# Sample tile in pairs and quads of 128-column chunks per PSUM bank, and one PSUM bank held back instead of two, in a four-layer hybrid decoder step

## The chip, the cores and the metric

The kernel runs on all 8 cores of one Trainium2 chip. Each core holds one prompt of 2048 positions and one tile of 128 sample positions (16 sequences of 8). The cores do not talk to each other. The time of a run is the device time of its slowest core, in microseconds (us).

A run has a state. In the fast state all cores have about the same granted TensorE clock (in nearly all of them 0.985 to 0.994 of full speed). In the slow state the cores of one die, sometimes of both, have a lower one, here down to 0.81, and the run is some per cent longer. I use a second figure, called the **die median** below: of every run, take each die (cores 0 to 3, 4 to 7) whose four cores all had a granted clock above 0.985, take the median span of its four cores, and then the median over all such dies. An undisturbed die in a slow run is as good as one in a fast run: of the kernel before, 28 dies of fast runs have a median of 6847.9 us, and 15 undisturbed dies of slow runs one of 6847.5. For the kernel before, this figure came out as 6847.1, 6847.7, 6847.0 and 6850.8 us (8 to 12 dies each, three chips), so it repeats within 4 us, 0.06%.

## The reference

Each of 4 layers does this, for the prompt and for the sample alike:

```python
h = rmsnorm(x, n1) * (1 + sc1) + sh1
x = x + 0.5 * gt1 * swiglu(h, f1g, f1u, f1d)            # "FFN1", width 2816
h = rmsnorm(x, nm) * (1 + sc2) + sh2
xp, xl, gl, u, v, gates = split(h @ w_in)
y_pool = pool_mixer(xp)                                  # windows 2, 4, 8, 16
y_lru  = rg_lru(causal_conv(xl)) * gelu(gl)              # conv of width 4, gates, a recurrence
y_gm   = chunk_gmlp(u, v)                                # positions mixed in chunks of 128
g = sigmoid(gates)
x = x + gt2 * ((g0*(y_pool@wbo_pool) + g1*(y_lru@wbo_lru) + g2*(y_gm@wbo_gmlp)) @ w_out)
h = rmsnorm(x, n2) * (1 + sc3) + sh3
x = x + 0.5 * gt3 * swiglu(h, f2g, f2u, f2d)            # "FFN2"
```

A last RMSNorm follows. The model width is 1024, which the kernel holds as 8 chunks of 128 channels on the partitions, with the positions along the free axis. The new states of pooling, conv, RG-LRU and gMLP are outputs too.

## The kernel before

The work comes in two passes. The first takes half of the prompt, the second takes the other half with the sample tile riding along:

```python
GROUPS = [
    [TT_("p", 0, 512, 0), TT_("p", 512, 512, 512)],
    [TT_("p", 0, 512, 1024), TT_("p", 512, 512, 1536), TT_("s", 1024, 128, 0)],
]
```

The kernel declares its PSUM buffer as `[P, 8, 512]` in fp32, and its planner hands it out as 8 banks of 512 values. A prompt tile has 512 columns and fills one bank. A sample tile has 128 columns and leaves three quarters of its bank empty. This is what the FFN does for each of 22 hidden chunks and for every tile, the sample included:

```python
def unit(wb, jb, ji, t):
    ...
    pg, pu = PV(), PV()                       # two banks
    acc(pg.c(n), [(g[:, k, ji * P:(ji + 1) * P], hT[:, k, t.cols]) for k in range(KC)], n)
    acc(pu.c(n), [(u[:, k, ji * P:(ji + 1) * P], hT[:, k, t.cols]) for k in range(KC)], n)
    sg = SB()
    act(sg.f(n), pg.c(n), AF.Silu)
    tt(hid(jb * 2 + ji)[:, t.cols], sg.f(n), pu.c(n), ALU.mult)
```

The branch gates, the pooling input, the down and output projections with their residual, and the RMSNorm sums follow the same pattern: one chunk, one bank, one ACT and one DVE instruction. The two gates of an RG-LRU chunk take a bank each:

```python
for t in grp:                                  # in Lru.gates
    pr, pi = PV(), PV()
    acc(pr.c(n), [(wr_, hb.b(n, t.col))], n)
    acc(pi.c(n), [(wi_, hb.b(n, t.col))], n)
    act(self.ab.f(n, t.col), pr.c(n), AF.Tanh, bias=lruc[:, l, 2, ch:ch + 1], scale=0.5)
    act(self.ib.f(n, t.col), pi.c(n), AF.Tanh, bias=lruc[:, l, 3, ch:ch + 1], scale=0.5)
```

No engine's order is written by hand. When the program is built, a planner plays the whole program through with cost figures of its own, and each time an engine is free it takes the first instruction, in program order, that is ready *and fits*. `fits` decides on PSUM banks and on pages of a scratch area in SBUF. The order on each engine, the banks and the pages are then fixed for good. These are the parts that the argument touches:

```python
SEM_LAT = 70.0                                 # planner: end of an instruction to its dependant, ns

def place(vb):                                 # a run of free scratch pages of 64 floats
    ...
    down = not w and vb.nu <= 9                # small buffers from the top, larger ones from below
    ...

def fits(o):
    ...
    if need and len(banks) < need + (0 if first else 2):
        return False                           # an instruction out of turn must leave 2 banks free
    ...
```

`first` is true where the instruction's bank is the next in program order. An instruction that is not the next one may only take a bank if two more stay free. In the trace every TensorE instruction (PE) has the one source line of the helper that recorded it, L623, or L624 after the change; DVE and ACT lines are those of helpers likewise. Groups are therefore told apart by their operands: `R` are the large activations (FFN hidden, pooled and gated branches), `mem` is scratch or weights, `onesb` is the ones matrix of the norm sums.

Of the kernel before, what the change touches and what calls it, by code (L numbers as in the profile page):

```python
# [13 lines left out]
ALU = mybir.AluOpType  # L14
# [19 lines left out]
LRU_LEAD = 1.3  # L34

# [92 lines left out]
class Sched:  # L128
# [103 lines left out]
    def schedule(self):  # L232
# [60 lines left out]
        def fits(o):  # L293
# [9 lines left out]
            if need and len(banks) < need + (0 if first else 2):  # L303
                return False
# [206 lines left out]
def build_nc():  # L511
# [306 lines left out]
    class Norm:  # L818
# [8 lines left out]
        def chunk(self, m):  # L827
            t, n = self.t, self.t.n
            x = self.x(m)
            if m == 0:  # L830
                self.sum = SB(n)
                act(self.sum.f(n), x, AF.Square)
            else:
                sq = SB(n)
                act(sq.f(n), x, AF.Square)
                if m < KC - 1:
                    tt(self.sum.f(n), self.sum.f(n), sq.f(n), ALU.add)
                else:
                    tot = SB(n // 2)
                    tt(tot.b(n), self.sum.f(n), sq.f(n), ALU.add)  # L840
                    mm([(self.pv.c(n), onesb[:], tot.b(n), True, True)], n)
            self.k += 1
# [28 lines left out]
    def final_norm(nm):  # L871
        t, n = nm.t, nm.t.n
        r = nm.rstd()
        for k in range(KC):
            y = SB()
            stt(y.f(n), xT[:, k, t.cols], vecT[:, V_NF + k:V_NF + k + 1], r.f(n), ALU.mult, ALU.mult)
            if t.kind == "p":
                dma(y_p[:, k, t.pos0:t.pos0 + n], y.f(n))
            else:
                dma(y_s[:, k, :], y.f(n))  # L880

    def resid(l, wh, m, t, pv):
        n = t.n
        xs_ = xT[:, m, t.cols]
        if t.kind == "p":
            stt(xs_, pv.c(n), modp(l, wh, m), xs_, ALU.mult, ALU.add)
        else:
            tmp = SB()
            g3 = modT[:, l % 2, wh * 8 + m, 1:17].unsqueeze(2).to_broadcast([P, NSEQ, TSAMP])
            tt(tmp.f(n).rearrange("p (s t) -> p s t", t=TSAMP),  # L890
               pv(lambda b: b[:, 0:n].rearrange("p (s t) -> p s t", t=TSAMP)), g3, ALU.mult, n=n)
            tt(xs_, xs_, tmp.f(n), ALU.add)
# [5 lines left out]
    def ffn(l, which, grp, after, between=None, begin=None):  # L898
# [4 lines left out]
        def unit(wb, jb, ji, t):  # L903
            n = t.n
            g = w3(wb[:, 0:2048], KC)
            u = w3(wb[:, 2048:4096], KC)
            pg, pu = PV(), PV()
# [25 lines left out]
        def down(wb, m, t):  # L933
            n = t.n
            w = w3(wb, NJ)
            py = PV()
            acc(py.c(n), [(w[:, j, :], hid(j)[:, t.cols]) for j in range(NJ)], n)
            resid(l, wh, m, t, py)
            norms[id(t)].chunk(m)

        for m in range(4):
            v = wload(dn[l, m], NJ * P)
            for t in grp:
                down(v, m, t)
            hook()
# [3 lines left out]
        for t in grp:  # L949
            for m in range(4, KC):  # L950
                down(vs[m - 4], m, t)
            after(norms[id(t)])


    def gate_unit(l, br, wblk, nk, m, grp, src):
# [3 lines left out]
        tot = sum(t.n for t in grp)  # L959
        sg = SB(tot)  # L960
        for t in grp:
            n = t.n
            pp, pg = PV(), PV()
# [4 lines left out]
            if br == 0:  # L968
                stt(merged[:, m, t.cols], s_, 1.0, pp.c(n), ALU.add, ALU.mult)
            else:  # L970
                stt(s_, s_, 1.0, pp.c(n), ALU.add, ALU.mult)
        if br != 0:
            mg = merged[:, m, 0:tot]
            tt(mg, mg, sg.f(tot), ALU.add)

    def window(d, x, w, carry, smp=False):

        n = NSEQ * 23 if smp else NPR
        pick = (lambda a: a.rearrange("p (s x) -> p s x", s=NSEQ)[:, :, 15:23]) if smp else (lambda a: a)
        m = P if smp else NPR  # L980
# [16 lines left out]
    def pool_unit(l, g, grp, wblk, gi):  # L997
        wv = wblk
        w = 2 << g
        last = gi == len(GROUPS) - 1  # L1000
        wx = w3(wv[:, 0:2048], KC)
        for c in range(2):
# [7 lines left out]
            xs = None  # L1010
            for t in grp:
                n = t.n
                pb = PV()
                acc(pb.c(n), [(wx[:, k, c * P:(c + 1) * P], hT[:, k, t.cols]) for k in range(KC)], n)
                if t.kind == "p":
                    act(x[:, 16 + t.col:16 + t.col + n], pb.c(n), AF.Copy)
                else:
                    xs = SB(16 + NSEQ * 23)
                    x3 = xs.f(NSEQ * 23, 16)
                    memset(xs.f(16), 0.0)  # L1020
                    dma(x3, spool_d[l, ch])
                    act(x3.rearrange("p (s x) -> p s x", s=NSEQ)[:, :, 15:23],
                        pb(lambda b: b[:, 0:P].rearrange("p (s x) -> p s x", s=NSEQ)), AF.Copy, n=n)
                    dma(o_pool_s[l, ch], x3)
# [5 lines left out]
            if xs is not None:  # L1030
                window(ybr[:, ch, NPR:NPR + P].rearrange("p (s x) -> p s x", s=NSEQ), xs.f(16 + NSEQ * 23), w, False, True)
# [3 lines left out]
    class Lru:  # L1035
# [9 lines left out]
        def gates(self):  # L1045
# [37 lines left out]
            for t in grp:  # L1083
                n = t.n
                pr, pi = PV(), PV()
                acc(pr.c(n), [(wr_, hb.b(n, t.col))], n)
                acc(pi.c(n), [(wi_, hb.b(n, t.col))], n)
                act(self.ab.f(n, t.col), pr.c(n), AF.Tanh, bias=lruc[:, l, 2, ch:ch + 1], scale=0.5)
                act(self.ib.f(n, t.col), pi.c(n), AF.Tanh, bias=lruc[:, l, 3, ch:ch + 1], scale=0.5)
# [37 lines left out]
    def gm_v(l, t, sub, wblk):  # L1127
# [10 lines left out]
        act(vnb, pv.c(512), AF.Copy, scale=sm[:, 1:2])  # L1138
        if t.kind == "s":
# [3 lines left out]
            dma(o_v_s[l], vf.f(512))  # L1143

    def gm_u(l, t, g, wblk):
        n = t.n
        nsub = n // P
        wu3 = w3(wblk, KC)
        wm = wsp[:, g if t.kind == "p" else 4 + g, :]
        px = PV()  # L1150
        mm([(px(lambda b, s=s: b[:, s * P:(s + 1) * P]),
             vnT[:, (t.col + s * P) * 4 + g * P:(t.col + s * P) * 4 + (g + 1) * P], wm, True, True)
            for s in range(nsub)], P)
        sb_ = SB()
        b3 = bsb[:, 0 if t.kind == "p" else 1, g, :].unsqueeze(1).to_broadcast([P, nsub, P])
        stt(sb_.f(n).rearrange("p (s x) -> p s x", x=P), px(lambda b: b[:, 0:n].rearrange("p (s x) -> p s x", x=P)),
            vcol(l, "gn", g), b3, ALU.mult, ALU.add, n=n)
        pu = PV()
        acc(pu.c(n), [(wu3[:, k, g * P:(g + 1) * P], hT[:, k, t.cols]) for k in range(KC)], n)
        tt(ybr[:, g, t.cols], pu.c(n), sb_.f(n), ALU.mult)  # L1160

    def mixer(l, grp, gi, after):
# [66 lines left out]
        for g in range(4):  # L1229
            for t in grp:  # L1230
                fg.append((2.0 * t.n / 512, lambda t=t, g=g: u_f(t, g)))
# [22 lines left out]
        for t in grp:  # L1254
            nm = Norm(t)
            for m in range(KC):
                n = t.n
                py = PV()
                wo = w3(wos[m // 2], KC)
                acc(py.c(n), [(wo[:, k, (m % 2) * P:(m % 2 + 1) * P], merged[:, k, t.cols]) for k in range(KC)], n)  # L1260
                resid(l, 5, m, t, py)
# [28 lines left out]
    def first_norm(grp, x=None):  # L1290
        for t in grp:
            nm = Norm(t, x)
            for m in range(KC):
# [163 lines left out]
```

## Time and profile before

The kernel before took 6863.71 us (median of 3 runs, 6861.04 to 7466.54). Its profiled run fell in the slow state. These are lines of the profile's list of cores, before:

```profile
core 5: 6834.7 us, clock 0.989
die 0 (median of its cores): 7025.1 us, clock 0.958
die 1 (median of its cores): 6847.9 us, clock 0.988
```

Die 1 was undisturbed, so all that follows is read from core 5. This is its busy line from the profile page (busy time, share of the span, instructions), and the line of the page for the slowest core that says which engine the chain that ended last ran through:

```profile
PE 6608.6 (97%) x37553; PEld 3221.1 (47%) x37553; DVE 3000.5 (44%) x4419; ACT 2481.4 (36%) x3988; POOL 659.6 (10%) x1257
PE 88%; issue 4%; DVE 3%; ACT 2%; DMA 2%; POOL 1%; SPq 0%; DVEq 0%; ACTq 0%; POOLq 0%
```

TensorE bounds the kernel, and DVE and ACT are less than half busy on average. I therefore looked for a gain only where PE is idle. The next fence shows layer 2 of the second pass in three stretches of the windows view, core 5, before: the mixer with its output projection, FFN2, and FFN1 of the next layer. The cuts are at the norm-sum matmuls of those boundaries.

```profile
core 5: us, PE busy (x) PEld busy (x) DVE busy (x) ACT busy (x) POOL busy (x), PEclk, DMA share, GB/s
4403.60:4754.30 350.70, 327.18 (x1927) 164.57 (x1926) 223.60 (x301) 170.30 (x282) 59.91 (x102) 0.97 0.40 77
4754.30:5013.00 258.70, 255.70 (x1547) 130.88 (x1546) 83.31 (x158) 67.17 (x124) 9.51 (x18) 0.99 0.35 64
5013.00:5299.10 286.10, 286.10 (x1785) 148.49 (x1784) 96.47 (x177) 85.72 (x149) 14.87 (x32) 1.00 0.40 74
```

In FFN1 the PE is busy in 286.10 of 286.10 us. In FFN2 it loses 3.0 us, all at its start. The mixer loses 23.5 us, with DVE at 64% and ACT at 49%.

The ends of matmuls are modelled, which hides short gaps: a 128-column matmul is shown as 220 ns long, while the next one starts 56 ns after it. I therefore also sum, over the second pass, how much later each matmul starts after the one before it than at full rate. Full rate is what the trace shows within runs of matmuls: 216 ns between starts for 512 columns, 56 ns for 128 (the small 17-column ones, which occur in the first pass only, are counted at 30 ns, though most follow at 25). I call that sum the **excess**. Before, it was 172.8 us for the second pass on core 5.

These are the largest waits of the PE for ACT or DVE in the second pass, before (columns: engine, its line, what was waited for; us in total, times, longest):

```profile
PE psum L623 <- ACT mem L645: 59.2, 49, 4.7
PE psum L623 <- DVE R L653: 24.6, 12, 3.7
PE psum L623 <- DVE mem L653: 21.9, 7, 7.3
```

The longest wait of the first line, 4.7 us, is not in a mixer. It stands in the FFN1 at the start of the second pass (PE timeline, before, window 3262:3284):

```profile
3276.11 8.26 PE L623 MATMUL psum<-hT,mem 128*128 128x512 bf16 x36 [4.75 <-ACT mem L645]
```

There an ACT eviction of the sample tile had waited 10.5 us for a transfer of first-pass results (`y_p`), and for some 6 us after the wait the matmuls started 427 ns apart (mean granted clock 0.57 between 3276 and 3283 us). The excess of this place is 7.7 us, called the **stall at the start of the pass** below.

What one instruction of the sample tile costs is in the list of groups by shape, before (count | busy us, mean ns | idle before it). The first two lines are a sample chunk's eviction on ACT and a sample chunk's product on DVE, the third is the same product of a prompt tile, and the last counts the table loads of ACT:

```profile
L645 ACT ACTIVATE mem<-psum 128x128 f32<-128x128 f32 x381 | 107.0, 283 | 357.4 <-PE psum L623 323.2 <-DVE R L653 14.4 <-DMA y_p<-mem 10.5
L653 DVE TENSOR_TENSOR R<-mem,psum 128x128 bf16<-128x128 f32 x176 | 50.7, 288 | 56.2 <-PE psum L623 30.3 <-ACT mem L645 25.7
L653 DVE TENSOR_TENSOR R<-mem,psum 128x512 bf16<-128x512 f32 x704 | 483.2, 688 | 1857.7 <-PE psum L623 1754.1 <-ACT mem L645 103.3
L645 ACT ACT_TABLE_LOAD x257 | 329.7, 1283 | 206.9 <-PE psum L623 172.6 <-DVE small L653 9.0 <-DVE R L653 5.4
```

A product of 128 columns takes 288 ns and one of four times as many takes 688. If a straight line joins the two, some 155 ns of each are fixed: an estimate. The same estimate for ACT, from 283 ns for 128 columns and 598 for 512 (`ACTIVATE mem<-psum 128x512`, x1524), is some 178 ns. Two waits repeat in each of the four mixers. The first is the PE's timeline at the start of FFN2, before (start us, duration us, instruction, count, and in brackets the idle time before it with its releaser):

```profile
4754.49 13.65 PE L623 MATMUL psum<-R,mem 128*128 128x512 bf16 x104
4771.14 0.59 PE L623 MATMUL psum<-mem,onesb 128*128 128x512 bf16 x1 [3.00 <-DVE mem L653]
```

After the last output projection (104 matmuls), the PE waits 3.00 us until DVE has added up the squares for the norm. The second is the PE's timeline where the gMLP branch meets the RG-LRU gates, before:

```profile
4600.26 0.22 PE L623 MATMUL psum<-wsp,R 128*128 128x128 bf16 x1
4604.19 1.97 PE L623 MATMUL psum<-mem 128*128 128x512 bf16 x5 [3.70 <-DVE R L653]
```

A position-mixing matmul of the sample (`wsp`) is followed by 3.70 us of nothing before the matmuls of the RG-LRU gates.

### The profile page before, as it was taken

The numbers are of one execution on the slowest core, as the hardware profiler recorded it, in microseconds if no ns is written. First come the engines' busy times: TensorE is split into PE (matmuls) and PEld (weight loads), VectorE is DVE, ScalarE is ACT, GpSimd is POOL, SyncE is SP. The second block draws the span as 40 slices with busy tenths as digits, with TensorE's granted clock in tenths as the row PEclk, the third lists the DMA queues.
The fourth block names the chain that finished last, engine by engine and source line by source line (L and its number), as shares of the span: only waits on it lengthen the run. The fifth ranks groups of instructions, "written<-read, shape, count | busy, mean of one in ns | idle before, by whom it ended". The sixth has DMA issues, their size and how long they took to land.

```text
span 7032.5 us, 105309 instructions; the slowest of 8 cores (6834.7 to 7032.5 us)
## 1 busy us (share of the span) xinstructions
PE 6808.5 (97%) x37553; PEld 3267.9 (46%) x37553; DVE 3001.3 (43%) x4419; ACT 2478.3 (35%) x3988; POOL 654.7 (9%) x1257
## 2 busy tenths in 40 slices
PE   7999999999999999999999999999999999999999
PEld 3434444444444444444454455544455444554444
DVE  2254321653327422653427533275332754327543
ACT  3253221542226312543326332164321543215431
POOL 0011000110002000110002100011000110001100
PEclk8878888999999999999999999999999999999999
DMA  6566545665555556554634334343333333344333
GB/s 125 85 109 101 90 80 96 111 105 100 103 104 107 95 93 120 108 96 82 143 57 97 69 59 80 62 86 70 66 71 74 79 72 66 63 77 86 70 63 71
DMA packets 165357, 613.90 MB, mean 87 GB/s; under 512 B 22128, under 2 KB 58224, under 8 KB 125424
## 3 DMA queue, kind: packets, MB, share of 16 engines
q0 software_dynamic: 101376, 530.62, 43.4%
q1 hardware_dynamic: 63472, 76.55, 3.7%
q8 instruction: 312, 5.11, 0.3%
q14 instruction: 197, 1.61, 0.1%
HBM read 1103.15 MB, written 30.34 MB: 161 GB/s over the span
## 4 chain that ended last, share of the span: by engine, by line
PE 88%; issue 4%; DVE 3%; ACT 2%; DMA 2%; POOL 1%; SPq 0%; DVEq 0%; ACTq 0%; POOLq 0%
PE psum L623 88%; ACT mem L645 1%; DVE mem L690 1%; DMA mem<-ada_w 1%; DVE mem L668 1%; DMA mem<-ffn_gu 1%; ACT L645 1%; DMA mem<-w_v 0%; DVE mem L653 0%; POOL small L653 0%; DMA y_p<-mem 0%; DVE R L668 0%; DVE R L653 0%; ACT R L645 0%; POOL small L661 0%
## 5 line engine op out<-in xcount | busy, mean ns | idle before, releaser
L623 PE MATMUL psum<-hT,mem 128*128 128x512 bf16 (+1 forms) x22400 | 4398.5, 356 | 50.7 <-ACT mem L645 37.0
L623 PEld LDWEIGHTS psum<-hT,mem 128*128 128x128 bf16 x22400 | 2041.0, 100 | 2271.3 <-issue 535.2
L623 PE MATMUL psum<-R,mem 128*128 128x512 bf16 (+1 forms) x11520 | 2269.3, 354 | 41.9 <-ACT mem L645 17.7
L645 ACT ACTIVATE mem<-psum 128x512 f32<-128x512 f32 (+1 forms) x1969 | 1023.9, 536 | 2989.9 <-PE psum L623 2744.4
L623 PEld LDWEIGHTS psum<-R,mem 128*128 128x128 bf16 x11520 | 1049.1, 99 | 1177.9 <-issue 240.6
L653 DVE TENSOR_TENSOR R<-mem,psum 128x512 bf16<-128x512 f32 (+1 forms) x880 | 533.6, 607 | 2010.2 <-PE psum L623 1887.6
L645 ACT ACTIVATE mem<-xT 128x512 f32<-128x512 f32 (+1 forms) x504 | 279.2, 561 | 1121.8 <-DVE xT L668 1065.0
L668 DVE SCALAR_TENSOR_TENSOR xT<-psum,modT,xT 128x512 f32<-128x512 f32 x384 | 286.2, 750 | 728.5 <-PE psum L623 728.3
L645 ACT ACT_TABLE_LOAD x257 | 329.7, 1283 | 235.5 <-PE psum L623 181.1
L668 DVE SCALAR_TENSOR_TENSOR mem<-mem,psum 128x512 f32<-128x512 f32 x320 | 194.0, 607 | 457.2 <-PE psum L623 454.3
L653 DVE TENSOR_TENSOR mem<-mem 128x512 f32<-128x512 f32 (+3 forms) x471 | 284.7, 612 | 201.3 <-ACT mem L645 193.3
L698 POOL DMA_DIRECT2D mem<-ffn_gu x176 | 93.0, 529 | 2399.3 <-PE psum L623 2335.9
L645 ACT ACTIVATE hT<-mem,modT 128x512 bf16<-128x512 f32 x384 | 276.1, 801 | 52.1 <-DVE mem L653 33.1
L668 DVE SCALAR_TENSOR_TENSOR mem<-mem,vecT 128x1024 f32<-128x1024 f32 (+1 forms) x288 | 273.2, 974 | 8.0
L653 DVE TENSOR_TENSOR mem<-xT,mem 128x512 f32<-128x512 f32 x392 | 252.0, 688 | 52.1 <-ACT mem L645 42.6
L668 DVE SCALAR_TENSOR_TENSOR mem<-mem 128x1024 f32<-128x1024 f32 (+1 forms) x128 | 163.8, 1285 | 194.2 <-ACT mem L645 193.9
L645 ACT ACTIVATE mem<-mem 128x512 f32<-128x512 f32 (+3 forms) x209 | 187.5, 899 | 10.4 <-DVE R L653 4.2
L698 POOL DMA_DIRECT2D mem<-ffn_dn x128 | 67.6, 529 | 1279.8 <-PE psum L623 1261.7
L645 ACT ACTIVATE mem<-psum,lruc 128x128 f32<-128x128 f32 (+1 forms) x320 | 172.4, 631 | 39.3 <-DVE mem L690 15.7
L653 DVE TENSOR_TENSOR R<-R,mem 128x1024 bf16<-128x1024 bf16 (+1 forms) x128 | 165.3, 1291 | 13.6 <-DVE mem L668 0.9
L645 ACT ACTIVATE mem<-mem,lruc 128x1024 f32<-128x1024 f32 (+1 forms) x128 | 165.5, 1293 | 10.4 <-DVE mem L668 6.3
L690 DVE TENSOR_TENSOR_SCAN mem<-mem,lrust 128x1024 f32<-128x1024 f32 (+1 forms) x64 | 158.8, 2481 | 3.6 <-DVE mem L653 0.3
(77 smaller groups left out, 1959.4 us busy)
## 6 DMA issues: line engine op xcount, KB each, us to landing
mem<-ffn_gu POOLq DMA_DIRECT2D x176, 1024.0 KB, 9.5
mem<-ffn_dn POOLq DMA_DIRECT2D x128, 704.0 KB, 6.9
mem<-ada_w POOLq DMA_DIRECT2D x72, 1024.0 KB, 10.2
mem<-w_gate POOLq DMA_DIRECT2D x32, 1024.0 KB, 10.0
mem<-w_gate POOLq DMA_DIRECT2D x32, 768.0 KB, 8.3
mem<-w_lru POOLq DMA_DIRECT2D x64, 320.0 KB, 7.1
mem<-w_pool POOLq DMA_DIRECT2D x32, 512.0 KB, 9.4
mem<-w_lru POOLq DMA_DIRECT2D x64, 256.0 KB, 9.2
```

What stands on the lines that cost most here:

```text
L623: ins = e.matmul(res(o), lhsT=res(l), rhs=res(r), start=st, stop=sp)
L645: return S.add("act", lambda e: e.activation(out=res(out), in_=res(in_), func=func, **kw), reads=rd, writes=wr, cost=cost, tset=TSETS.get( ...
L653: return S.add(eng, lambda e: e.tensor_tensor(out=res(out), in0=res(in0), in1=res(in1), op=op), reads=[in0, in1], writes=[out], cost=dcost(n))
L668: return S.add(eng, lambda e: e.scalar_tensor_tensor(out=res(out), in0=res(in0), scalar=scalar, in1=res(in1), op0=op0, op1=op1), reads=rd, ...
L690: return S.add("dve", lambda e: e.tensor_tensor_scan(out=res(out), data0=res(d0), data1=res(d1), initial=init, op0=op0, op1=op1), reads=rd ...
L698: return S.add(q, lambda e: e.dma_start(out=res(out), in_=res(in_), **kw), reads=[in_] if reads is None else reads, writes=[out] if writes ...
```

## The change

The intent is twofold. First, the sample tile is worked on two chunks at a time (or two gates and two values, or all four gMLP groups), side by side in one PSUM bank, and one ACT and one DVE instruction evict them together. The matmuls stay as they were; ACT and DVE instructions get fewer, and banks are held by fewer tiles. Second, an instruction out of turn may take a bank if one other stays free, not two.

```diff
+RESERVE = 1
-            if need and len(banks) < need + (0 if first else 2):
+            if need and len(banks) < need + (0 if first else RESERVE):
 ...
@@ the norm's sum of squares
         def chunk(self, m):
+            c = 1 if t.kind == "p" else 2
+            x = self.x(m) if c == 1 else xT[:, m:m + 2, t.cols]
 ...           # squares and sums c*n columns at a time; the last step:
-                    mm([(self.pv.c(n), onesb[:], tot.b(n), True, True)], n)
+                    mm([(self.pv.c(n), onesb[:], tot.b(n, i * n), i == 0, i == c - 1) for i in range(c)], n)
@@ FFN unit
+            if t.kind == "s":
+                if ji == 0:
+                    return
+                pv = PV()                                     # ONE bank: g0 g1 u0 u1
+                mm([(pv(lambda b, i=i, h=h: b[:, (2 * h + i) * P:(2 * h + i + 1) * P]), w[:, k, i * P:(i + 1) * P],
+                     hT[:, k, t.cols], k == 0, k == KC - 1)
+                    for i in range(2) for h, w in enumerate((g, u)) for k in range(KC)], n)
+                sg = SB(2 * n)
+                act(sg.f(2 * n), pv.c(2 * n), AF.Silu)
+                tt(RB[(2, 1, 0)[j // 8]][:, j % 8:j % 8 + 2, t.cols], w3(sg.f(2 * n), 2),
+                   pv(lambda b: b[:, 2 * n:4 * n]...), ALU.mult)
+                return
@@ gate_unit: the same for gate and value of two chunks (one bank, not four);
@@ prompt merges of branches 1 and 2 no longer contain the sample's columns
-            mg = merged[:, m, 0:tot]
-            tt(mg, mg, sg.f(tot), ALU.add)
+            mg = merged[:, m, 0:NPR]
+            tt(mg, mg, sg.f(NPR), ALU.add)
@@ pool_unit, resid: two sample chunks in one bank, one window()/residual chain for both
+            pb = project(2 * g, t, ...)
+            act(x4[:, :, :, 15:23], pb(...), AF.Copy, n=2 * P)
+            window(ybr[:, 2 * g:2 * g + 2, t.cols]..., xs.f(16 + 2 * nx), w, False, True)
@@ Lru.gates
+                else:
+                    pv = PV()                                 # both gates in one bank
+                    pr, pi = pv.c(n), pv(lambda b: b[:, P:2 * P])
+                    mm([(pr, wr_, hb.b(n, t.col), True, True), (pi, wi_, hb.b(n, t.col), True, True)], n)
@@ gm_u: all four groups of the sample at once, two banks in all
+            mm([(q(px, i), vnT[...], wsp[:, 4 + i, :], True, True) for i in range(4)], P)
+            tt(sb_.f(512), px.c(512), bsb[:, 1].rearrange("p g t -> p (g t)"), ALU.add)
@@ last norm of the sample: two halves of four chunks, 2 output DMAs, not 8
```

Cut here: the output and down projections (through `project`), the sample's v chain, which gets one more ACT copy, and the loops that step by two.

## The prediction

> **What bounds it now.** Two fast runs agree (6861, 6864 us). The profile fell in the slow state, so I read core 5 of the undisturbed die (6834.7 us, clock 0.989). TensorE bounds it: PE busy 97%, chain of waits 88% PE. In the timeline matmuls start every 216 ns (512 columns) or 56 ns (128), back to back. 28,116 and 7,132 of those plus 2,304 small ones make about 6530 us (an estimate from these durations); the change leaves that stream as it is. So at most 300 us can be won, some 60 of it at start and end.
>
> Where the rest is (busy times by stretch):
> - Second pass, where the sample tile rides along, FFN stretches: PE 530.0 of 530, 535.0 of 535. Nothing to win there.
> - The four mixers of that pass: PE 335 of 360 us each, DVE 232, ACT 187: 25 us idle each, 102 in all. Start-to-start excess over 216/56 ns is larger (modelled ends hide part): about 165 us for the pass.
> - First pass after its start: about 28 us of PE idle.
>
> PE waits in these mixers: RG-LRU gate matmuls behind table load and Tanh evacuations (1.9, 0.5, 0.5 us: banks), 2.8 us of a sample projection for a bank, 4.4 and 3.8 us for ACT/DVE around further LRU steps, 2.4 us before the output projection (last merge), 3.2 us before a norm-sum matmul.
>
> **What the change does.**
> - Halves sample instructions: 128-column ops take 288 ns (DVE) and 283 ns (ACT), 512-column ones 687 and about 600, so about 155/175 ns are fixed. Pairing saves an estimated 40 to 45 us of DVE and of ACT over the pass, but two thirds of it in FFNs and projections, where PE never waits. [...]
> - Frees banks: a sample pair of gates takes one bank, not four; LRU sample gates one, not two. [...]
> - RESERVE 1 lets later PE work go ahead with two free banks instead of three. In the instruction order, 24 FFN matmuls (5.2 us) now stand before the norm-sum matmul after the output projection, none before: the 3.2 us wait should go. Prompt merges no longer include sample columns, so the sample's 32 matmuls (1.8 us) cover most of the 2.4 us wait.
> - Adds a longer sample v chain (one more ACT copy) and later sample results: covered by prompt work.
>
> The LRU/pool section stays DVE bound (84 of 100 us in its first stretch); its scans, convs and 1152-column ops are untouched, so part of the waits stays.
>
> **Sum.** Mixers of pass 2: 5 us each from the two boundary waits, 6 to 10 each from banks and order: 45 to 60. First pass, RESERVE: 5 to 10. Last norm (2 output DMAs, not 8): 2 to 4. Total about 65 us, 0.95%.
>
> Predicted 6798 us, 8 in 10 within 6745 to 6848. Faster by over 2%: 0.10; within 2%: 0.88; slower: 0.02.
>
> **What would show it.** FFN stretches still at 100% PE; PE idle of a pass-2 mixer down from 25 to about 12 us; ACT and DVE busy down about 40 us each without a matching gain; norm-sum and output-projection waits gone, LRU gate waits partly left; first pass nearly the same.
>
> **What would make it wrong.** The new order may place LRU gate matmuls earlier and stall PE on DVE (no gain); or banks may be the real limit throughout the mixers, and nearly all 165 us go (over 2%).

45 to 60, 5 to 10 and 2 to 4 us make 52 to 74, stated as about 65. The fixed 155 and 175 ns are an estimate from the times of two sizes, on each engine, that stand beside them. That four 128-column results go into one bank is the kernel's own layout (4 x 128 of the bank's 512 values). The terms for the first pass and the last norm are estimates, for which no measured number was given.

## The result

The changed kernel took 7181.01 us as the median of 4 runs (6774.51 to 7463.55), but three of those four were slow, and the interval below rests on the fast one and on a fifth, also fast (6782.06 us); the kernel before took 6866.77 us beside it (4 runs, 6861.04 to 7466.54). Ratios are computed as the mean time of one kernel's fast runs over that of the other's of the same rounds, so they are not quite the ratio of the medians quoted. The ratio of fast runs is 0.9874, with a 95% interval of 0.9845 to 0.9903: about 86 us less, and within 2%. The die median went from 6847.1 to 6765.5 us, 82 us less. The lists of cores and the busy line of core 5, after:

```profile
core 5: 6772.4 us, clock 0.991
die 1 (median of its cores): 6760.9 us, clock 0.992
PE 6588.5 (97%) x37566; PEld 3217.7 (48%) x37566; DVE 2967.3 (44%) x4107; ACT 2483.3 (37%) x3812; POOL 668.2 (10%) x1241
```

DVE lost 312 instructions and 33 us. ACT lost 176 instructions and *gained* 2 us. The chain that ended last, after (profile page of the slowest core), has two points more of PE:

```profile
PE 90%; issue 3%; DMA 3%; DVE 2%; ACT 2%; POOL 1%; SPq 0%; DVEq 0%; ACTq 0%; POOLq 0%
```

The same three stretches of layer 2, from the windows view of core 5, after:

```profile
4390.90:4729.30 338.40, 323.03 (x1927) 163.56 (x1926) 221.87 (x283) 171.55 (x269) 53.90 (x97) 0.97 0.41 81
4729.30:4982.00 252.70, 252.70 (x1547) 130.05 (x1546) 79.63 (x129) 69.06 (x111) 9.50 (x18) 1.00 0.35 65
4982.00:5268.30 286.30, 286.30 (x1787) 148.65 (x1786) 93.28 (x148) 82.66 (x132) 15.74 (x33) 1.00 0.39 72
```

A layer of the second pass went from 895.5 to 877.4 us: 12.3 us in the mixer, 6.0 us in FFN2, nothing in FFN1. FFN1 lost 29 of 177 DVE instructions and 17 of 149 ACT instructions, and took the same time, since PE was at 100% before and after. Four such layers make 72 us.

The excess of the second pass fell from 172.8 to 98.7 us, by 74.1. The excess of the first pass did not fall in these two traces (94.9 before, 102.4 after, both on core 5). At the end of the program, the PE waits 7.4 us before the last norm sum and 7.3 us pass after the last matmul; after the change these are 7.9 and 7.7. So the second pass's mixers and their borders are most of the gain that can be placed, 66.8 of the 74.1 us by the table below. The other 7.3, in the column "rest", are in the main the stall at the start of the pass. A wait like it stands on all eight cores of the profile before (4.75 to 8.67 us), and on none of the profile after. The experiments do not take it apart further.

One trace cannot place the 82 us more closely. Core 5 itself became only 62.3 us shorter, since its first pass had 7.5 us more of excess and its first matmul came 3 us later. In the repeat e5, core 5 has 92.3 us of excess in the second pass and 92.2 in the first and took 6755.2 us, 79.5 less than before. So the first pass differs by 10 us between two runs of the same kernel; in fast runs the cores of one kernel differ by about 30 us among each other.

Of the largest waits of the PE for ACT or DVE in the second pass, after:

```profile
PE psum L624 <- ACT mem L646: 46.5, 24, 7.2
PE psum L624 <- DVE mem L654: 7.8, 1, 7.8
PE psum L624 <- DVE R L654: 4.4, 12, 0.7
```

The 12 waits on `DVE R` shrank from 24.6 to 4.4 us, and of those on `DVE mem L653/L654` only the last of the program is left. The waits on `ACT mem` halved in number, but the longest is now 7.2 us, where it had been the 4.7 of the stall. That one is new.

At the start of FFN2, PE timeline after:

```profile
4729.53 14.10 PE L624 MATMUL psum<-R,mem 128*128 128x512 bf16 x112
4743.46 5.34 PE L624 MATMUL psum<-hT,mem 128*128 128x512 bf16 x24
4748.64 0.38 PE L624 MATMUL psum<-mem,onesb 128*128 128x512 bf16 x1
```

Now 24 matmuls of the FFN, 5.34 us, stand ahead of the norm sum, and no idle time is shown before it. Where gMLP meets the RG-LRU, PE timeline after:

```profile
4583.65 0.39 PE L624 MATMUL psum<-wsp,R 128*128 128x128 bf16 x4
4583.87 3.62 PE L624 MATMUL psum<-hT,mem 128*128 128x512 bf16 x16
4587.99 0.38 PE L624 MATMUL psum<-mem 128*128 128x512 bf16 x1 [0.28 <-DVE mem L669]
```

The four sample groups are done at once, 16 projection matmuls (3.62 us) fill the time that had been idle, and waits of 0.28 us are left in place of the 3.70.

And this is the new wait, as the timelines of PE, DVE and ACT have it, after:

```profile
4430.93 1.54 DVE L669 SCALAR_TENSOR_TENSOR R<-mem 128x256 bf16<-128x256 f32 x2
4431.52 1.28 ACT L646 ACT_TABLE_LOAD   x1 [6.37 <-DVE R L669]
4432.81 0.69 ACT L646 ACTIVATE mem<-psum,lruc 128x512 f32<-128x512 f32 x1
4433.64 1.56 PE L624 MATMUL psum<-mem 128*128 128x512 bf16 x3 [7.18 <-ACT mem L646]
```

PE waits 7.18 us for a bank. The bank comes free by a Tanh on ACT, which waited 6.37 us for DVE, and then loaded its table. DVE had in the meantime ended a prompt chunk's pooling (1.22 us), scanned a *pair* of sample chunks (1.69) and a prompt chunk (2.33), and then made the last step of the pair (the 128x256 instruction, line 669), for which ACT waited. This occurs in every mixer of the second pass. In the program's recorded dependences, the Tanh does not need the pooled values at all: its output had been placed on scratch pages which that pair's buffer had just used.

Last, the groups by shape, after. Evictions of sample pairs on ACT, products of sample pairs on DVE, and table loads:

```profile
L646 ACT ACTIVATE mem<-psum 128x256 f32<-128x256 f32 x152 | 58.7, 386 | 355.1 <-PE psum L624 349.5 <-DVE R L654 5.0 <-DMA mem<-spool 0.6
L654 DVE TENSOR_TENSOR R<-mem,psum 128x256 bf16<-128x256 f32 x88 | 37.0, 420 | 141.8 <-ACT mem L646 141.8
L646 ACT ACT_TABLE_LOAD x285 | 365.7, 1283 | 198.0 <-PE psum L624 132.1 <-DVE R L669 27.1 <-DVE small L654 9.0
```

A pair costs 386 ns on ACT where two singles cost 2 x 283 = 566, and 420 ns on DVE where two cost 2 x 288 = 576. So the instructions did become cheaper by 180 and 156 ns per pair, close to the estimates of the fixed part (178 and 155). But the new order makes ACT switch tables 28 times more often, and 28 x 1.283 = 36 us of loads ate ACT's saving. From the end of the ACT instruction before a load to the start of the one after it, the median over the 284 loads of this trace that have both is 1.31 us.

### The profile page after: what moved, and what is told of

It reads as the page before. It is cut to its first block, busy times and chain, and to the rows that moved or that the text cites. A ratio compares the mean times of both kernels' runs of the same rounds, so it can differ in the third digit from the quotient of the medians.

```text
span 6773.2 us, 103563 instructions; the slowest of 8 cores (6742.9 to 6773.2 us)
## 1 busy us (share of the span) xinstructions
PE 6583.4 (97%) x37566; PEld 3216.3 (47%) x37566; DVE 2969.0 (44%) x4107; ACT 2483.2 (37%) x3812; POOL 673.1 (10%) x1241
## 4 chain that ended last, share of the span: by engine, by line
PE 90%; issue 3%; DMA 3%; DVE 2%; ACT 2%; POOL 1%; SPq 0%; DVEq 0%; ACTq 0%; POOLq 0%
PE psum L624 90%; DMA mem<-ffn_gu 1%; ACT mem L646 1%; DMA mem<-ada_w 1%; DVE mem L669 1%; POOL small L654 0%; DMA wc_d<-mem 0%; DVE mem L691 0%; DVE R L669 0%; ACT R L646 0%; ACT L646 0%; DVE R L654 0%; POOL small L662 0%; DMA mem<-w_gate 0%; POOL mem L675 0%
## 5 line engine op out<-in xcount | busy, mean ns | idle before, releaser
L624 PE MATMUL psum<-hT,mem 128*128 128x512 bf16 (+1 forms) x22400 | 4246.0, 349 | 58.0 <-ACT mem L646 28.7
L624 PEld LDWEIGHTS psum<-hT,mem 128*128 128x128 bf16 x22400 | 2007.0, 98 | 2165.3 <-issue 100.7
L624 PE MATMUL psum<-R,mem 128*128 128x512 bf16 (+1 forms) x11520 | 2198.7, 347 | 11.8 <-DVE R L654 7.9
L646 ACT ACTIVATE mem<-psum 128x512 f32<-128x512 f32 (+3 forms) x1817 | 1000.0, 566 | 2841.8 <-PE psum L624 2673.4
L624 PEld LDWEIGHTS psum<-R,mem 128*128 128x128 bf16 x11520 | 1031.2, 98 | 1098.5 <-issue 20.1
L654 DVE TENSOR_TENSOR R<-mem,psum 128x512 bf16<-128x512 f32 (+1 forms) x792 | 519.8, 658 | 1927.3 <-PE psum L624 1666.1
L654 DVE TENSOR_TENSOR mem<-mem 128x512 f32<-128x512 f32 (+3 forms) x419 | 278.1, 665 | 235.8 <-ACT mem L646 228.4
L654 DVE TENSOR_TENSOR mem<-xT,mem 128x512 f32<-128x512 f32 x394 | 252.2, 688 | 55.3 <-ACT mem L646 46.7
L646 ACT ACTIVATE mem<-mem 128x512 f32<-128x512 f32 (+3 forms) x209 | 187.4, 898 | 12.6 <-DVE R L654 4.2
L646 ACT ACTIVATE mem<-psum,lruc 128x512 f32<-128x512 f32 (+1 forms) x320 | 175.5, 630 | 31.1 <-PE psum L624 15.8
L654 DVE TENSOR_TENSOR R<-R,mem 128x256 bf16<-128x256 bf16 (+1 forms) x160 | 170.0, 1065 | 14.9
```

The source lines that it names most:

```text
L624: ins = e.matmul(res(o), lhsT=res(l), rhs=res(r), start=st, stop=sp)
L646: return S.add("act", lambda e: e.activation(out=res(out), in_=res(in_), func=func, **kw), reads=rd, writes=wr, cost=cost, tset=TSETS.get( ...
L654: return S.add(eng, lambda e: e.tensor_tensor(out=res(out), in0=res(in0), in1=res(in1), op=op), reads=[in0, in1], writes=[out], cost=dcost(n))
```

## The experiments

All runs gave correct outputs, and all were compared with the kernel before on the same chip. The table gathers the die medians, with their change against the kernel before in the same batch (for the changed kernel, which was run first, that of the first batch), and the excess of the second pass on core 5, split by where it lies: at the output projection and the norm sum, in the gMLP part, in the part with pooling and the RG-LRU (the first half of a mixer), and the rest.

| kernel | die median, us (dies) | change | norm sum, out. proj. | gMLP | pooling, RG-LRU | rest | sum |
|---|---|---|---|---|---|---|---|
| before | 6847.1 (12) | | 30.9 | 52.9 | 76.4 | 12.6 | 172.8 |
| after | 6765.5 (6) | -82 | 3.1 | 28.9 | 61.4 | 5.3 | 98.7 |
| e5: after, again | 6765.2 (6) | -82 | 2.9 | 25.2 | 56.9 | 7.4 | 92.3 |
| e1, e11: pairs only | 6788.1 (5), 6789.8 (2) | -59 | 3.1 | 53.4 | 50.5 | 5.4 | 112.4 |
| e2: reserve only | 6811.1 (9) | -36 | 25.5 | 59.8 | 45.6 | 9.0 | 139.9 |
| e3: after, pooling single | 6790.2 (8) | -57 | 3.1 | 34.7 | 71.9 | 15.6 | 125.3 |
| e4: after, other placement | 6788.8 (7) | -58 | 3.1 | 38.4 | 67.8 | 16.3 | 125.6 |
| e6: pairs in two banks | 6819.8 (6) | -28 | 3.5 | 31.8 | 112.3 | 5.3 | 152.9 |
| e7: one bank, singles | 6796.8 (4) | -51 | 3.1 | 25.4 | 87.1 | 15.4 | 131.0 |
| e8: after, conv on ACT | 6762.6 (6) | -85 | 3.1 | 38.0 | 51.5 | 5.3 | 97.9 |
| e9: hybrid | 6792.5 (9) | -55 | 3.1 | 38.6 | 54.6 | 27.7 | 124.0 |
| e10: complement of e9 | 6816.2 (5) | -31 | 21.1 | 54.7 | 58.8 | 13.0 | 147.6 |
| e12: after, later handover | 6767.8 (7) | -83 | 3.1 | 13.0 | 53.1 | 24.3 | 93.5 |

The excess agrees with the die medians: their changes differ by at most 11 us in any row. Parts of the excess are single observations of one core. The rows "after" and "e5" are two runs of the same kernel, and differ by 6 us in the sum and by up to 4.5 in a part; differences of that size are not read. (The row of e5 was computed later than the others, from its trace; the cuts used for it give the other rows within about 1 us.)

### e1 and e11: the pairs alone; e2: the reserve alone

The theory of the prediction was that pairs and reserve do different things: the reserve lets the PE run ahead at the norm sum, and the pairs give banks and DVE time back in the mixers. The rival was that one of the two does nearly all.

```diff
-RESERVE = 1                                   # e1 and e11: the changed kernel
+RESERVE = 2
```
```diff
-            if need and len(banks) < need + (0 if first else 2):    # e2: the kernel before
+            if need and len(banks) < need + (0 if first else 1):
```

For e1:

> The changed kernel with RESERVE back at 2: pairs and quads alone. Theory A (freed banks: one bank where a sample pair took two or four, and a better instruction order, carry the gain; RESERVE adds little): ratio to before 0.989 to 0.993, mixers of the second pass within 4 us of the changed kernel's, the 3.2 us norm-sum wait still gone (the order still has 24 FFN matmuls in front of it). Rival B (RESERVE 1, the run-ahead, carries the gain): ratio 0.996 to 1.000.

For e2:

> The kernel before with RESERVE 1 alone, sample work unpaired. Theory A: ratio 0.995 to 0.999 and most of the 25 us of PE idle per second-pass mixer stay. Rival B: ratio 0.987 to 0.991.

The profile of e1 fell in the slow state, and only one of its runs was fast (6801.65 us), so there is no ratio. The same kernel was looked at again as e11, and that profile is fast:

> Pairs with RESERVE 2 once more (die median 6788 in the first batch), for a profile in the fast state, which the first one was not. If RESERVE 1 is worth 23 us on top of pairs by letting PE run ahead in the pooling/RG-LRU section, that section has 20 us or more per mixer here against 15, and gMLP, output projection and norm sum are as in the changed kernel within 1 us.

Measured: pairs only, die median 6788.1 us (5 dies, 6785.6 to 6791.1), 59 us less than before. Reserve only, 6811.1 us (9 dies, 6806.6 to 6814.8), 36 us less, with a ratio of fast runs of 0.9963 (0.9946 to 0.9981). Both together give 82, somewhat less than 59 + 36 = 95. Neither does nearly all, though both figures lie in the ranges of theory A (6788.1 is 0.9914 of the time before), and rival B's fit neither. The expectation for e11 failed: the pooling and RG-LRU part has 12.6 us per mixer there and not 20 or more, and gMLP 13.4 where the changed kernel has 7.2.

But the roles were not those of the prediction. The columns of the table show it:

- The wait at the norm sum and the output projection is gone with the pairs alone (3.1 us left of 30.9), and stays with the reserve alone (25.5). With the pairs and the old reserve, the same 24 FFN matmuls stand ahead of the norm sum. So it is the pairs, and not the reserve, that remove this wait.
- The gMLP part needs both: 53.4 with the pairs, 59.8 with the reserve, 28.9 with both, 52.9 before.
- The part with pooling and RG-LRU improves more with either alone (50.5, 45.6) than with both (61.4 and, in e5, 56.9). The new wait of 7.2 us does not explain this, for it comes with the pairs: e11 has it in every mixer too, at 7.0 us, and e2, with the reserve alone, has it in none (in layer 2 the longest wait at this place is 2.61 us). Why the part is longer with both was not found.

For the first and the third point, these are lines of the PE's timeline of the pairs-only kernel (e11), the FFN matmuls ahead of the norm sum at the start of FFN2 and the new wait in the mixer before it:

```profile
4745.42 5.34 PE L624 MATMUL psum<-hT,mem 128*128 128x512 bf16 x24
4432.35 1.17 PE L624 MATMUL psum<-mem 128*128 128x512 bf16 x2 [6.96 <-ACT mem L646]
```

For the second point, this is the PE's timeline of the pairs-only kernel (e11) where gMLP meets the RG-LRU:

```profile
4580.65 0.39 PE L624 MATMUL psum<-wsp,R 128*128 128x128 bf16 x4
4583.47 0.99 PE L624 MATMUL psum<-mem 128*128 128x512 bf16 x3 [2.43 <-DVE mem L675]
```

The four sample groups come together, as in the changed kernel, but no projection matmuls follow them, and the PE waits 2.43 us for DVE. With the reserve at 1, the planner puts 16 projection matmuls there.

### e5: the change again

> The changed kernel itself once more, as a control on the same chip as the next three. Times are compared by the median span of the cores of a die at full granted clock (about 0.99), because slow runs are frequent: on the chip of the first four experiments that is 6848 us for the kernel before in every undisturbed die, 6789 for pairs alone, 6811 for RESERVE 1 alone, 6789 with pooling unpaired and 6788 with the 12-page limit. Expected here: 6760 to 6770 for the changed kernel and 6845 to 6852 for before. If it comes out at 6788 instead, the 27 us between it and the variants were the chip's, not theirs.

The changed kernel ran once more, beside e6 to e8 and on the chip of e1 to e4: ratio 0.988 (0.9834 to 0.9927), die median 6765.2 us. The result stands, and the die medians of both sets of runs (6765.5 and 6765.2 us) agree within 1 us.

### e3 and e4: is the new wait an accident of scratch placement?

The recorded dependences suggested a theory, called S in what follows: the new wait comes from where the planner puts scratch. A pair of sample pooling chunks has a buffer of 752 floats, 12 pages. The limit for "small, from the top" is 9 pages, so the pair's buffer goes among the large ones, and the RG-LRU's Tanh output lands on its pages right behind it. A single chunk's buffer (6 pages) is placed from the top. If S holds, either unpairing the pooling alone (e3) or raising the limit to 12 pages (e4) should take the wait away and gain up to 29 us. The rival is that DVE is simply late at this place.

```diff
-            pb = project(2 * g, t, ...)                       # e3: the changed kernel with the
+            acc(pb.c(n), [(wx[:, k, c * P:(c + 1) * P], ...   # sample pooling of the kernel before
-            down = not w and vb.nu <= 9                        # e4: the changed kernel
+            down = not w and vb.nu <= 12
```

For e3:

> The changed kernel with the pooling branch of the sample tile unpaired again (two 368-column windows instead of one of 736). In the changed kernel each second-pass mixer has a new PE wait of 7.3 us at RG-LRU gate matmuls, behind an ACT table load that waits for the DVE window of a sample pooling pair. Theory S (scratch: the paired window buffers take 12 pages, over the limit of 9 for the end of scratch where small buffers go, so RG-LRU tiles are put on their pages and wait for their last reader): the 7.3 us wait goes or falls under 3 us, total 10 to 25 us shorter than the changed kernel, ratio to before 0.984 to 0.987. Rival D (DVE is simply behind there, whatever the buffers): the wait stays within 2 us of 7.3 and the time is equal or worse by the lost pairing, ratio 0.988 to 0.990.

For e4:

> The changed kernel with the limit for small scratch buffers at 12 pages instead of 9, so that the paired pooling buffers go to the small end as the single ones did; no instruction is added or removed. Theory S: the 7.3 us wait falls under 3 us in each of four mixers, total 10 to 25 us under the changed kernel, ratio to before 0.984 to 0.987. Rival D: the wait stays, ratio 0.987 to 0.989.

Measured: e3 6790.2 us (8 dies, 6787.2 to 6800.4), e4 6788.8 us (7 dies; ratio of fast runs 0.9911, 0.9887 to 0.9934). Both are some 24 us *slower* than the changed kernel, and slower than either forecast (D's ended at 0.990; e3's die median is 0.9917 of the time before). In e3 the 7.2 us are gone as well, with the pairs; its longest waits in this part are 6.0 us for DVE's line 675 and 3.8 for ACT. For e4, the PE timeline shows why the dependence was not the cause that matters:

```profile
4425.83 3.61 PE L624 MATMUL psum<-hT,mem 128*128 128x512 bf16 x16 [0.67 <-ACT mem L646]
4436.01 0.59 PE L624 MATMUL psum<-mem 128*128 128x512 bf16 x1 [6.56 <-DVE mem L675]
```

The dependence on the pair's pages is gone, and the PE still waits 6.56 us at this place, now for DVE's conversion of the conv output to bf16 (line 675), before which DVE had been busy without a break. S named the last releaser rightly, but as an explanation of the lost time it fell: behind one releaser stood the next. The test is not a clean one, though: the planner made another order for e4, in which this conversion ends at 4435.8 us, where in the changed kernel it ends at 4425.8. The gap of the changed kernel, 7.2 us in every mixer of the second pass, had a buffer as its last releaser; but giving the buffer another place (e4) did not shorten the kernel.

Why pairing the pooling is worth 25 us here (e3 against the changed kernel) remains open. It is not the new wait. The table says only where the time is: of 27 us of excess that e3 has more, 10 are in the pooling and RG-LRU part, 6 in gMLP and 10 in the rest, where the PE waits for FFN weights (`DMA mem<-ffn_gu`, 6.1 us in e3, 5.8 in e4; none on core 5 in the second pass of the changed kernel).

### e6 and e7: banks or instructions?

The pairs do two things at once: half as many ACT and DVE instructions, and fewer banks. The bank theory says that the banks make the gain, the instruction theory that the instructions do. e6 keeps every paired instruction but spreads the halves of the FFN and branch-gate pairs over two banks and the two RG-LRU gates too. e7 keeps the banks of the change but evicts 128 columns at a time, with 4002 ACT and 4479 DVE instructions in the trace (changed kernel 3812 and 4107, kernel before 3988 and 4419).

```diff
-                pv = PV()                                       # e6, FFN unit; the gates likewise
-                mm([(pv(... (2 * h + i) * P ...)) ... for h, w in enumerate((g, u)) ...], n)
+                pv, pv2 = PV(), PV()
+                for q, w in ((pv, g), (pv2, u)):
+                    mm([(q(lambda b, i=i: b[:, i * P:(i + 1) * P]), ...) for i in range(2) for k in range(KC)], n)
-                act(sg.f(2 * n), pv.c(2 * n), AF.Silu)          # e7, FFN unit; all others likewise
+                for i in range(2):
+                    act(sg.f(n), pv(lambda b, i=i: b[:, i * n:(i + 1) * n]), AF.Silu, n=n)
```

For e6:

> The changed kernel with the same paired ACT and DVE instructions, but the halves of FFN pairs, gate pairs and RG-LRU gates in two PSUM banks each instead of one. Theory A (freed banks carry the gain of pairing): most of the pairing gain is lost, die median 6795 to 6815. Rival C (fewer ACT and DVE instructions, of which the mixer's DVE is short, carry it): die median within 10 us of the changed kernel.

For e7:

> The changed kernel with its matmul groups and banks, two or four sample results in one bank, but ACT and DVE working on each 128 columns by themselves as before (about 200 ACT and 370 DVE instructions more than the changed kernel, about 40 us of ACT and 50 us of DVE busy time). Theory A: die median within 12 us of the changed kernel. Rival C: 6795 to 6820.

Measured: e6 6819.8 us (6 dies, 6812.3 to 6827.7; ratio 0.9957, 0.9922 to 0.9992), e7 6796.8 us (4 dies, 6794.1 to 6806.9; ratio 0.994, 0.9888 to 0.9992). With the reserve alone the kernel was at 6811. So paired instructions with these three uses in two banks add nothing to the reserve, they even cost 9 us; single instructions in shared banks add 14 us; both together add 46. e6 came out near what the bank theory (A) had forecast, e7 within what the instruction theory (C) had. Neither is whole: fewer instructions paid here only where the banks were there too. But e7 also makes the pooling windows single, as e3 does, and that alone cost 25 us of the 31 that e7 lost; how little the other single instructions would cost by themselves was not tested.

The PE timeline of e6 shows what two banks do at the RG-LRU gates:

```profile
4454.79 0.59 PE L624 MATMUL psum<-mem 128*128 128x512 bf16 x1 [0.99 <-ACT mem L646]
PE psum L624 <- ACT mem L646: 76.0, 72, 3.1
```

One gate matmul after another waits about 1 us for ACT to empty a bank (the next at 4456.36, again 0.99 us). The last line is from the view of waits over e6's second pass: 72 waits of the PE on ACT, where the changed kernel has 24. Its pooling and RG-LRU part has an excess of 112.3 us, against 61.4. Which of the three uses that were doubled (FFN pairs, branch gates, RG-LRU gates) is responsible was not told apart.

### e8: less DVE in the mixer

If DVE is late in the first half of the mixer, taking work off it should shorten that half. The conv's first product moves from DVE to ACT in both passes.

```diff
-                ts(out, x(0), cw(0), cw(4), ALU.mult, ALU.add, n=m)
+                act(out, x(0), AF.Identity, bias=cw(4), scale=cw(0), n=m)
```

> The changed kernel with the first product of each RG-LRU convolution on ACT instead of DVE: about 9 us of DVE work taken off each mixer, 10 us added to ACT. Reading to test: the waits left in the second-pass mixers (about 23 us each, 11 of them at the first RG-LRU gate matmuls) come from DVE being the busiest engine there, whatever scratch and banks are. Then these 11 us fall by 3 to 8 us per mixer and the die median is 10 to 30 us below the changed kernel's. If scratch or banks hold PE back, it moves by less than 8 us.

Measured: DVE busy fell from 2967.3 to 2910.5 us and ACT's rose from 2483.3 to 2563.0 us (core 5). The die median is 6762.6 us (6 dies, 6758.7 to 6781.3), 3 us less than the changed kernel's; the ratio of fast runs to the kernel before is 0.9925, with an interval from 0.9795 to 1.0056 that says nothing. The excess in the pooling and RG-LRU part did fall, from 61.4 (56.9 in e5) to 51.5, but that in the gMLP part rose by about as much, from 28.9 (25.2) to 38.0. The wait moved. So the reading that DVE is what limits there failed by its own forecast (10 to 30 us); a move of less than 8 us had been put down to scratch or banks.

### e9 and e10: do the parts add?

e9 takes from each kernel the part that had looked better: the changed kernel, but with pooling, RG-LRU gates and branch-0 gates of the sample as singles, since the reserve alone had had only 45.6 us of excess there. e10 is the opposite: the kernel before with the reserve at 1, and pairs in just those three places. Theory L said that a mixer's parts are local, so that their excess adds; the rival, that the planner's order couples them.

```diff
-            if t.kind == "s":                  # e9, branch-0 gates; pooling and RG-LRU gates likewise
+            if t.kind == "s" and br != 0:
-            gate_unit(l, br, ...)              # e10, the kernel before with reserve 1
+            (gate_unit if br else gate_unit0)(l, br, ...)     # gate_unit0: the paired one
```

For e9:

> The changed kernel with the sample work of the pooling and RG-LRU section single again (pooling units, RG-LRU gates, gates of the pooling branch), everything else paired, RESERVE 1. Per second-pass mixer the matmuls' start-to-start excess in that section is 19 us in the kernel before, 7 with RESERVE 1 alone, 15 in the changed kernel; in the gMLP part 13, 14 and 7.5; at the output projection and norm sum 8, 6 and 1. Theory L (each section's waits come from that section's own form: pairs pay in gMLP, output projection and norm sum, and cost 8 us against singles in the pooling/RG-LRU section): this kernel has 7 to 9 us in the section and die median 6730 to 6745, under both kernels. Rival M (the static order is made as a whole and the sections do not add): the section has 15 us or more, die median 6765 or more.

For e10:

> The opposite half: the kernel before with RESERVE 1 and pairs only in the pooling and RG-LRU section. Theory L: about 15 us in that section per mixer, the waits at gMLP, output projection and norm sum as with RESERVE 1 alone, die median 6830 to 6850, so above RESERVE 1 alone (6811). Rival M: anything else; at or under 6811 if the pairs of this section help.

Measured: e9 6792.5 us (9 dies; ratio 0.9923, 0.9894 to 0.9951), so 27 us slower than the changed kernel. Its excess in the pooling part was 54.6 us, 13.6 in each mixer, where theory L had expected 7 to 9. And a wait arose where there had been none, in the FFN, from the view of waits over its second pass:

```profile
PE psum L624 <- DMA mem<-ffn_gu: 17.0, 3, 9.7
```

Three times the PE waits for FFN weights, up to 9.7 us. That is most of the loss: of 25 us of excess more than in the changed kernel, 22 are in the rest. e10 came to 6816.2 us (5 dies, 6810.0 to 6823.4; no ratio for want of fast runs), below the 6830 to 6850 expected of it. Part by part it is near what a sum has: at the norm sum (21.1) and in gMLP (54.7) close to the reserve alone (25.5, 59.8), in the pooling part (58.8) close to the changed kernel (61.4). The new wait is there too, 7.17 us in the mixer of layer 2, so it comes with the pairs of this part. So e10 alone doesn't tell against theory L, but on e9 it fell: parts that had looked better elsewhere were not so in another whole, and a part that nobody had touched got worse.

### e12: a planner that expects later handovers

In the changed kernel's trace, a PE that waits for ACT or DVE starts mostly 145 ns after the instruction that it waited for has ended (median 144 ns after ACT, 146 after DVE; nine in ten under 260, the longest 449). The planner assumes 70. With a larger figure it should order less tightly.

```diff
-    SEM_LAT = 70.0
+    SEM_LAT = 200.0
```

> The changed kernel with one constant of its planner changed: a result is taken to reach another engine 200 ns after its producer ends instead of 70. In the changed kernel's trace the step from the end of an ACT or DVE instruction to the matmul that waited for it is mostly 145 ns, up to 260. No instruction is added or removed; in the second pass's PE order, 8 more projection matmuls (1.7 us) now stand before the first RG-LRU gate matmuls of a mixer and 24 to 32 more before the first product with the pooled rows, and the gMLP and norm-sum order stays. Reading to test: what is left of the waits is PE reaching RG-LRU gates before DVE and ACT have delivered, as the planner's order has them too early. Then the pooling/RG-LRU section falls from 15 us per mixer to 8 to 12, gMLP and norm sum stay within 1.5 us, die median 6735 to 6757. Rival: order is not what limits there, the DVE is; then the wait only moves to the next DVE result, section 14 us or more, die median 6760 to 6785.

Measured: 6767.8 us (7 dies, 6763.7 to 6768.4; fast runs 6779.41 and 6781.47 us, no ratio), the same as the changed kernel. The forecast failed: 13.3 us per mixer in the pooling and RG-LRU part and not 8 to 12, gMLP not as it was, and the die median in the rival's range. Its mixer of layer 2, from the windows view, and two of its waits over the second pass:

```profile
4408.00:4741.30 333.30, 320.23 (x1935) 163.05 (x1934) 221.05 (x284) 168.48 (x268) 54.83 (x97) 0.99 0.42 83
PE psum L624 <- ACT mem L646: 46.3, 22, 7.0
PE psum L624 <- DMA mem<-ffn_gu: 13.9, 3, 7.0
```

The mixer took 333.3 us, 5.1 less than the changed kernel's 338.4, and its gMLP excess fell from 28.9 to 13.0. But the PE now waited 13.9 us for FFN weights, which gave it back. None of the twelve runs clearly beats the changed kernel.

## Why the prediction was right or wrong

The prediction of 6798 us (6745 to 6848) within 2% was right: it expected 65 us, and 82 (die median) to 86 us (ratio) came. Point by point:

- **PE bounds the kernel; the FFN has nothing to win.** Right for the stretches that it looked at. The FFN1 stretch took 286.1 us before and 286.3 after, at 100% PE both times, though DVE lost 29 instructions there and ACT 17. It missed the stall at the start of the pass, which is in an FFN1 and went with the change (7.7 us on core 5).
- **The gain lies in the second pass's mixers and their borders.** Right: of 82 us, some 67 to 75 are found there (66.8 by the excess of the two traces, 75 by that of e5, 72 by the windows of layer 2). This is the mis-sized term: the sum gave it 45 to 60. Of its parts, the two boundary waits were put at 5 us per mixer, 20 in all, and the excess at the norm sum and output projection fell by 27.8; banks and order were put at 24 to 40 in all, and the excess fell by 24.0 in gMLP and by 15.0 in the pooling and RG-LRU part, together 39 (47 in e5).
- **PE idle of a mixer from 25 to about 12 us.** Nearly: 23.5 to 15.4 us in layer 2 by the windows.
- **RESERVE lets FFN matmuls go ahead of the norm sum.** The wait went as predicted, but the step named the wrong cause. With the pairs and the old reserve the same 24 matmuls stand there and the excess is 3.1 us; with the reserve alone it is 25.5. The instruction order of the changed kernel showed that the wait would go, but not which half of the change moved it. Building each half alone and comparing the orders, without a run, would have told.
- **ACT and DVE busy down about 40 us each.** DVE fell by 33. ACT did not fall (2481.4 to 2483.3), since the new order has 28 more table loads of 1.283 us. The estimate counted instructions and forgot that an order decides how often ACT switches.
- **First pass, RESERVE: 5 to 10 us.** No gain is seen: its excess was 94.9 before and 102.4 after, but 92.2 in the repeat e5, so that a gain of 5 us would not show in one trace. The reserve-only kernel's total gain (36 us) is nearly that of its second pass (33 us of excess).
- **Last norm: 2 to 4 us.** Nothing: the two stretches at the end went from 7.4 and 7.3 to 7.9 and 7.7 us. The total was thus partly luck: the mixers gave more than they were given in the sum, the stall was not in it, and two terms of 7 to 14 us together did not show.
- **The RG-LRU and pooling section stays DVE bound, and part of its waits stays.** Right in that waits stay (61.4 of 76.4 us of excess). The prediction's warning that a new order may stall PE there came true within the gain: 7.2 us per mixer, which come with the pairs (e11, e10) and not with the reserve (e2). That section being bound by DVE is only half shown: taking 57 us of work off DVE (e8) shortened the section by 5 to 10 us but not the kernel.
- **Banks may be the limit throughout the mixers.** Partly: without the shared banks of FFN, branch gates and RG-LRU gates the pairs gave nothing beyond the reserve (e6), but with them 98.7 us of excess remain.

What is open: why paired pooling is worth 25 us when the placement theory fell, which of the bank uses undone in e6 matters, and how low the remaining 99 us could go with another order. Five of the experiments moved a wait elsewhere rather than removing it (e3, e4, e8, e9, e12), so a local edit's worth could not be read from the local wait.

## What to carry to other kernels

Pairing small tiles in one accumulation bank paid here where the matmul engine waited for a bank or for an evicting engine, and nothing where it was saturated, though FFN1 lost 29 DVE and 17 ACT instructions (286.1 us before, 286.3 after): nearly all of the gain came from the mixers, 40% of a layer. Shared banks and fewer instructions belonged together; beyond the looser bank rule, each alone (e6, e7) gave a third or less of what both gave. Run the changed kernel twice before reading a part of its trace: the two runs here differ by 6 us in the second pass's excess and 10 in the first's. Where a planner orders the whole program, compare the order of each half of a change alone before naming a cause, and count ACT's table switches in the new order, because they can eat what the evictions save (here 28 more loads of 1.283 us, 36 us in all).
